# Moving the split weight tiles of an encoder kernel to other byte positions in SBUF

## The chip, the core and the metric

The kernel runs on one core of one Trainium2 chip. The metric is the device time of one launch in microseconds. TensorE multiplies, VectorE (DVE) and ScalarE (ACT) do the elementwise work, GpSimd (POOL) does a few small operations and issues one kind of transfer, and SyncE (SP) issues nearly all transfers from HBM. SBUF, the on-chip memory, has 128 partitions; a tile has the same byte position in each of them, and these positions are what the change is about.

## The reference

The reference is a trunk of two layers over 256 tokens of width 2048. Each layer normalises, projects the tokens, runs 12 token-mixing heads and 4 heads of cross-attention into 256 memory tokens side by side, projects their joined output back, and adds it. Then comes a dense squared-ReLU MLP of width 8192. All of it is in float32.

```python
for i in range(2):
    n = rms_norm(h, attn_norm[i])
    z = n @ (a_w_in if i == 0 else b_w_in)          # 2048 -> 5120 or 3072
    mix = neighbourhood_attention(...) if i == 0 else gqa_block_attention(...)
    km, vm = split(m @ w_mem_kv[i])                  # m: normalised memory tokens
    cross = memory_attention(qm, km, vm)
    h = h + concat([mix, cross]) @ w_o[i]
    n = rms_norm(h, mlp_norm[i])
    h = h + square(relu(n @ w_up[i])) @ w_down[i]    # 2048 -> 8192 -> 2048
return rms_norm(h, final_norm)
```

## The kernel before

**Products in three.** TensorE multiplies in float32r here, which keeps fewer bits than float32. So each factor is split into a high part and the rest: `split` has ScalarE copy the source into a float32r tile (L301) and VectorE subtract the copy from the source (L302). A product of two such pairs is three matmuls, high by high, high by low and low by high, summed in PSUM. Every weight comes from HBM as raw float32 (`raw`, `raw_U`, `raw_T`, `b`, `t`), is split into two tiles, and is then read by TensorE.

**What streams and what stands still.** A matmul loads one operand of 128 by 128 into the array, where it stands still, and streams the other through it. There are four kinds of product:

- *S products* (`s_products`, L221 to L223): the weights stand still, and the 256 tokens of the input (`nT` or `memT`) stream. 256 columns each.
- *Up products* (`u_products`, L696 to L698): the same shape, with the MLP's input `hT` streaming and the weights `uh`, `ul` standing still. 3 × 2048 matmuls.
- *M products* (`m_products`, L209 to L213): the weights stream in 512 columns, and the input (`nT`, `memT`, `cat`, or the squared activations `a_p`) stands still.
- *Down products* (`run` in `down_grains`, L810 to L812): the activations `a_s` stand still and the weights stream, in 512 columns. Seven eighths of the down projection are done in pairs with seven products in place of eight: the first three take the split of `b` (`bh`, `bl`), the other four that of `t` (`th`, `tl`), whose blocks VectorE and an accumulating transfer from POOL's queue (L790) make by adding and subtracting. The last eighth (`plain_grains`) goes as M products.

The next operand to stand still is loaded while the present one is multiplied (PEld in the profile).

**Order.** The work is a list of grains, each with steps to load, to prepare and to split some grains ahead. `add_mlp` puts an up grain and a down grain in turn, so that VectorE's and ScalarE's splits run beside TensorE's matmuls. What comes out, for most of the MLP, is an alternation on TensorE: 48 up matmuls (two halves of 24, from two tiles of `uh` and `ul`), then 21 down matmuls. A scheduler orders the instructions of each engine when the program is built.

**Where the tiles stand.** A pool places its tiles one behind the other. `new_half` makes the split tiles of the S and M products from the pool `ring`: four of `hi`, four of `lo`, each `HALF + 64` floats long, of which a window of `HALF` floats (4096 bytes) is used. The window begins `STILL_AT` bytes into the tile for S products and at 0 for M products. `half_of_side` does the same for `uh` and `ul` from the pool `side`, two of each, with the window at `place` bytes: 0 for up products, `MOVING_AT` for the M products that use these tiles. A tile of `HALF + 64` floats is 4352 bytes, which is 256 more than a multiple of 512, so neighbours stand 256 bytes apart modulo 512. The pool `mlp` holds `z`, `c`, `a`, `bh`, `bl`, `th`, `tl`.

Of the kernel before, what the change touches and what calls it, by code (L numbers as in the profile page):

```python
# [10 lines left out]
F32 = mybir.dt.float32  # L11
F32R = mybir.dt.float32r
# [5 lines left out]
P = 128  # L18
# [16 lines left out]
HALF = CH // 2  # L35
# [3 lines left out]
STEPS = PK // 2  # L39
GUARD = 3  # L40

MOVING_AT = 160

STILL_AT = 64
MASKED = -1e30


# [27 lines left out]
def encoder_kernel(ctx: ExitStack, tc: tile.TileContext, t: dict, out: bass.AP):  # L75
    nc = tc.nc
# [3 lines left out]
    def opened(name, side="left", space=None, bufs=1):  # L80
        kw = {"space": space} if space else {}
        manager = tc.tile_pool(name=name, bufs=bufs, side=side, reuse_waits="tile", **kw)
        pools[name] = manager, manager.__enter__()
        return pools[name][1]
# [35 lines left out]
    for j in range(8):  # L120
        s = slice(j * 512, (j + 1) * 512)
        nc.sync.dma_start(mem0[:, s], t["memT"][:, s])
        if j % 2 == 0:
            s = slice(j * 256, (j + 2) * 256)
# [20 lines left out]
    def halves_of(w):  # L145

        tiles = {}

        def load():
            tiles["raw"] = loaded(w.src, "U")  # L150

        def prep_early(hf):
            tiles[hf] = half_of_side(tiles["raw"], hf, MOVING_AT)

        def prep(hf):
            if hf == 0:
                tiles["raw"] = at.ring.tile([P, CH], F32, tag="raw", bufs=3, name="raw")
                nc.sync.dma_start(tiles["raw"], w.src)
            tiles[hf] = new_half(w.kind)
            split(*tiles[hf], tiles["raw"][:, hf * HALF : (hf + 1) * HALF])  # L160

        def run(hf):
            if hf == 0:
                w.start(w)
            hi, lo = tiles.pop(hf)
            if w.kind == "S":
                s_products(w, hf * (KT // 2), KT // 2, hi, lo)
            else:
                for i in range(NT):
                    m_products(w, w.first + 2 * hf, 2, i, hi, lo, w.begins and hf == 0, w.last and hf == 1)  # L170

        def after():
            if w.last:
                w.done(w)
            if w.early == "last":
                to_work()

        if w.early:
            return [Grain(lambda: run(0), None, load, None, lambda: prep_early(0), SOON),
                    Grain(lambda: run(1), after, None, None, lambda: prep_early(1), SOON)]  # L180
        return [Grain(lambda: run(0), None, None, None, lambda: prep(0)),
                Grain(lambda: run(1), after, None, None, lambda: prep(1))]

    def new_half(kind):
        s = slice(STILL_AT // 4, STILL_AT // 4 + HALF) if kind == "S" else slice(0, HALF)
        return tuple(at.ring.tile([P, HALF + 64], F32R, tag=n, bufs=4, name=n)[:, s] for n in ("hi", "lo"))

    pin = tc.keep_in_program_order

# [109 lines left out]
    def split(dst_hi, dst_lo, src):  # L299

        first = nc.scalar.activation(dst_hi, src, AF.Copy)  # L301
        return first, nc.vector.tensor_tensor(dst_lo, src, dst_hi.bitcast(F32), op=ALU.subtract)  # L302
# [396 lines left out]

    def half_of_side(raw, hf, place=0):  # L700
        s = slice(place // 4, place // 4 + HALF)
        tiles = tuple(at.side.tile([P, HALF + 64], F32R, tag=n, bufs=2, name=n)[:, s] for n in ("uh", "ul"))
        box.setdefault("splits", []).append(split(*tiles, raw[:, hf * HALF : (hf + 1) * HALF]))
        return tiles

    def loaded(src, tag):
        raw = at.side.tile([P, CH], F32, tag=tag, bufs=2, name=f"raw_{tag}")
        nc.sync.dma_start(raw, src)
        return raw

    def up_grains(layer, part, m):
        own = {}

        def load():
            own["raw"] = loaded(t[f"w_up{layer}"][part * PK + m], "U")

        def prep(hf):
            own[hf] = half_of_side(own["raw"], hf)

        def run(hf):  # L720
            if hf == 0:
                if part == 0:
                    own["ps"] = at.acc.tile([P, 512], F32, tag="acc", name="ps_u")[:, :SEQ]
                else:
                    if part == 1 and m == 0:
                        closed("ps_att", "ps_acc")
                        at.sums = opened("ps_sums", space=bass.MemoryType.PSUM)
                        box["ps"] = {}
                    own["ps"] = at.sums.tile([P, 512], F32, tag="up", name="ps_u")[:, :SEQ]
            u_products(own["ps"], hf * (KT // 2), KT // 2, *own.pop(hf))  # L730

        def after():
            if part == 0 and m == 0:
                closed("cat", "ring")
                at.mlp = opened("mlp")
                box["z"] = [at.mlp.tile([P, 4, 512], F32, tag=f"z{q}", name=f"z{q}") for q in range(2)]
                box["z_set"] = set()
            squared(layer, part, m, own["ps"])

        return [Grain(lambda: run(0), None, load, None, lambda: prep(0), SOON),  # L740
                Grain(lambda: run(1), after, None, None, lambda: prep(1), SOON)]

    def squared(layer, part, m, ps):
# [23 lines left out]
    def down_grains(layer, part, n, begins, ends):  # L767

        q, j = part % 2 ^ n // STEPS, n % STEPS
        own = {}  # L770

        def load():
            src = t[f"w_pair{layer}"][(part * 2 + q) * STEPS + j]
            own["b"] = at.side.tile([P, 3 * 512], F32, tag="b", bufs=2, name="b")
            nc.sync.dma_start(own["b"], src[:, : 3 * 512])
            own["t"] = at.side.tile([P, 4, 512], F32, tag="T", bufs=2, name="t")
            nc.sync.dma_start(own["t"][:, 0, :], src[:, 3 * 512 :])

        def behind(fn):

            return (lambda: past(fn, box["splits"][-4])) if part == 0 and n < 2 else fn

        def block(k):

            return own["b"][:, k * 512 : (k + 1) * 512]

        def pre():
            s = own["t"]
            nc.vector.tensor_tensor(s[:, 1, :], s[:, 0, :], block(0), op=ALU.add)  # L789
            nc.gpsimd.dma_start(s[:, 0, :], block(1), accum_op=ALU.add)  # L790

        def prep_first():
            own["first"] = tuple(at.mlp.tile([P, 3 * 512], F32R, tag=x, name=x) for x in ("bh", "bl"))
            split(*own["first"], own["b"])

        def prep_second():
            s = own["t"]
            nc.vector.tensor_tensor(s[:, 2, :], s[:, 1, :], block(1), op=ALU.add)
            nc.vector.tensor_tensor(s[:, 3, :], s[:, 2, :], block(2), op=ALU.add)
            own["second"] = tuple(at.mlp.tile([P, CH], F32R, tag=x, name=x) for x in ("th", "tl"))  # L800
            split(*own["second"], s.rearrange("p a b -> p (a b)"))

        def run(which, products):
            hi, lo = own.pop(which)
            a = box["a", part, j]
            for name, ai, bi in products:
                if begins:
                    box["ps"][name] = at.sums.tile([P, 512], F32, tag=name, name=name)
                ps, s = box["ps"][name], slice(bi * 512, (bi + 1) * 512)
                nc.tensor.matmul(ps, a[:, 0, ai, :], hi[:, s], start=begins, stop=False)  # L810
                nc.tensor.matmul(ps, a[:, 0, ai, :], lo[:, s], start=False, stop=False)  # L811
                nc.tensor.matmul(ps, a[:, 1, ai, :], hi[:, s], start=False, stop=ends)  # L812

        def after(products):
            if ends:
                for name, _, _ in products:
                    taken(q, name)

        def after_second():
            after(SECOND)  # L820
            if ends:
                box["z_set"].add(q)
            if ends and (part, n) in FOLDS:
                folded(q)

        return [Grain(lambda: run("first", FIRST), lambda: after(FIRST), load, behind(pre), behind(prep_first), SOON),
                Grain(lambda: run("second", SECOND), after_second, None, None, behind(prep_second), SOON)]

# [35 lines left out]
    def plain_grains(layer, nb):  # L864
# [4 lines left out]
        own = {}  # L869
# [3 lines left out]

        def prep(c, hf):
            if c == 0:
                own[c, hf] = half_of_side(own[0], hf, MOVING_AT)
            else:
                own[c, hf] = tuple(at.mlp.tile([P, HALF], F32R, tag="bt"[hf] + x, name=f"{x}_p") for x in "hl")
                split(*own[c, hf], own[1][:, hf * HALF : (hf + 1) * HALF])
# [351 lines left out]
```

## Time and profile before

Three runs took 2053.01, 2053.34 and 2054.17 us, so the median is 2053.34. The page and the views are of one profiled execution.

| | before |
|---|---|
| median of the runs | 2053.34 us |
| span of the profiled execution | 2050.6 us |
| TensorE busy | 2028.0 us (99%) |
| weight loads busy | 1835.2 us (89%) |
| VectorE busy | 1657.1 us (81%) |
| ScalarE busy | 1242.0 us (61%) |
| GpSimd busy | 120.2 us (6%) |
| granted TensorE clock, mean | 0.998 |

The span runs from the first to the last instruction; what lies around it is not in the profile. A row of the groups names line, engine, operation, what is written and what is read, shapes and count; behind the bar stand the busy time in us, the mean of one in ns, and the idle time ahead of the group with what ended it. A row of the waits names who waited for whom: us in total, how often, and the longest. In the timeline a row is one instruction (or a few alike, with their count), with its start in us, its duration, the engine and the line. Matmuls are pipelined: one starts well before the one ahead of it has ended. The pace is therefore the difference between starts. In the view of stretches each row gives, behind the stretch and its length, the busy time and count of TensorE, weight loads, VectorE, ScalarE and GpSimd, then the granted clock, the busy share of the DMA engines and GB/s.

### The profile page before, as it was taken

What the parts mean: (1) busy time and instruction counts of PE and PEld (TensorE: products, weight loads), DVE (VectorE), ACT (ScalarE), POOL (GpSimd) and SP (SyncE); (2) the same over time, 40 slices, a digit from 0 to 9 for tenths busy, and PEclk for the clock granted to TensorE, in tenths of its full rate; (3) what the DMA queues carried; (4) which work ended last, traced back from release to release, by engine and by line L of the source; (5) the groups of instructions that cost most, each with busy time, mean ns of one, the idle gap of its engine ahead of it and who ended that gap; (6) DMA issues with size and microseconds to landing.
All of it is one profiled execution on the core that took longest, in us unless ns stands there. A gap on an engine that the chain in (4) does not pass through costs nothing.

```text
span 2050.6 us, 32620 instructions
## 1 busy us (share of the span) xinstructions
PE 2028.0 (99%) x13092; PEld 1835.2 (89%) x13092; DVE 1657.1 (81%) x2025; ACT 1242.0 (61%) x1616; POOL 120.2 (6%) x144
## 2 busy tenths in 40 slices
PE   8999999999999999999999999999999999999998
PEld 7899999889999999999988888889999999999996
DVE  6766666558998999989896667657989999999896
ACT  6645454556666666666655557556666666666664
POOL 0000000000000000000000001000000000000000
PEclk9999999999999999999999999999999999999999
DMA  7755555727777777777765554537878787777773
GB/s 280 284 190 180 189 175 178 275 86 224 234 228 232 218 238 230 220 234 226 232 219 204 178 180 144 195 115 224 242 223 237 215 243 220 232 226 228 231 220 134
DMA packets 93431, 433.84 MB, mean 212 GB/s; under 512 B 10464, under 2 KB 12128, under 8 KB 60128
## 3 DMA queue, kind: packets, MB, share of 16 engines
q1 hardware_dynamic: 75888, 399.25, 57.7%
q0 software_dynamic: 16816, 31.46, 8.7%
q8 instruction: 102, 1.67, 0.3%
q10 hardware_dynamic: 576, 1.05, 0.1%
q14 instruction: 49, 0.40, 0.1%
HBM read 398.17 MB, written 4.19 MB: 196 GB/s over the span
## 4 chain that ended last, share of the span: by engine, by line
PE 94%; DVE 3%; DMA 1%; ACT 1%; issue 1%; SPq 0%; POOLq 0%; POOL 0%; DVEq 0%; ACTq 0%
PE ps_u L698 11%; PE ps_u L696 11%; PE ps_u L697 11%; PE p L810 8%; PE p L811 8%; PE p L812 8%; PE ps_m L209 8%; PE ps_m L212 8%; PE ps_m L213 8%; PE ps_s L221 3%; PE ps_s L223 3%; PE ps_s L222 3%; DVE ul L302 1%; PE pt_a L378 1%; DVE tl L302 1%
## 5 line engine op out<-in xcount | busy, mean ns | idle before, releaser
L698 PE MATMUL ps_u<-hT,ul 128*128 128x256 f32 x2048 | 568.1, 278 | 2.4 <-DVE ul L302 2.3
L696 PE MATMUL ps_u<-hT,uh 128*128 128x256 f32 x2048 | 568.0, 277 | 0.1
L697 PE MATMUL ps_u<-hT,uh 128*128 128x256 f32 x2048 | 567.4, 277 | 0.0
L301 ACT ACTIVATE uh<-raw_U 128x1024 fp32r<-128x1024 f32 x278 | 294.6, 1061 | 303.5 <-PE ps_u L697 281.0
L302 DVE TENSOR_TENSOR lo<-raw,hi 128x1024 fp32r<-128x1024 f32 (+1 forms) x224 | 266.3, 1195 | 162.1 <-ACT hi L301 160.0
L698 PEld LDWEIGHTS ps_u<-hT,ul 128*128 128x128 f32 x2048 | 385.5, 188 | 5.2 <-DVE ul L302 4.2
L696 PEld LDWEIGHTS ps_u<-hT,uh 128*128 128x128 f32 x2048 | 384.9, 188 | 5.5 <-ACT uh L301 0.5
L697 PEld LDWEIGHTS ps_u<-hT,uh 128*128 128x128 f32 x2048 | 384.4, 188 | 4.6
L302 DVE TENSOR_TENSOR ul<-raw_U,uh 128x1024 fp32r<-128x1024 f32 x278 | 337.2, 1218 | 37.5 <-ACT uh L301 37.4
L301 ACT ACTIVATE hi<-raw 128x1024 fp32r<-128x1024 f32 (+1 forms) x224 | 231.8, 1040 | 215.9 <-PE ps_m L213 121.1
L301 ACT ACTIVATE th<-t 128x2048 fp32r<-128x2048 f32 x112 | 215.2, 1921 | 125.4 <-PE p L812 111.8
L302 DVE TENSOR_TENSOR tl<-t,th 128x2048 fp32r<-128x2048 f32 x112 | 256.1, 2286 | 26.4 <-ACT th L301 25.8
L302 DVE TENSOR_TENSOR bl<-b,bh 128x1536 fp32r<-128x1536 f32 x112 | 196.0, 1750 | 0.3 <-ACT bh L301 0.2
L811 PE MATMUL p<-tl,a_s 128*128 128x512 f32 x448 | 177.2, 395 | 0.0
L812 PE MATMUL p<-th,a_s 128*128 128x512 f32 x448 | 174.4, 389 | 0.0
L301 ACT ACTIVATE bh<-b 128x1536 fp32r<-128x1536 f32 x112 | 166.2, 1484 | 10.1 <-PE p L812 4.0
L810 PE MATMUL p<-th,a_s 128*128 128x512 f32 x448 | 166.1, 395 | 0.0
L790 POOL DMA_DIRECT2D t<-b x112 | 97.1, 867 | 1166.0 <-DVE t L789 593.6
L811 PE MATMUL p<-bl,a_s 128*128 128x512 f32 x336 | 131.0, 390 | 0.2 <-DVE bl L302 0.2
L812 PE MATMUL p<-bh,a_s 128*128 128x512 f32 x336 | 131.1, 390 | 0.0
L789 DVE TENSOR_TENSOR t<-t,b 128x512 f32<-128x512 f32 x112 | 77.2, 689 | 64.1 <-DMA t<-in_w_pair 52.5
L223 PE MATMUL ps_s<-nT,lo 128*128 128x256 f32 x448 | 124.9, 279 | 0.0
(233 smaller groups left out, 3813.4 us busy)
## 6 DMA issues: line engine op xcount, KB each, us to landing
raw_U<-in_w_up SPq DMA_DIRECT2D x128, 1024.0 KB, 6.6
b<-in_w_pair SPq DMA_DIRECT2D x112, 768.0 KB, 4.5
raw<-in_w_o SPq DMA_DIRECT2D x32, 1024.0 KB, 5.1
t<-in_w_pair SPq DMA_DIRECT2D x112, 256.0 KB, 3.5
t<-b POOLq DMA_DIRECT2D x112, 256.0 KB, 6.8
raw<-in_w_b SPq DMA_DIRECT2D x21, 1024.0 KB, 5.0
raw<-in_w_av SPq DMA_DIRECT2D x12, 1024.0 KB, 5.1
raw<-in_w_aq SPq DMA_DIRECT2D x12, 1024.0 KB, 5.0
```

Of the source, the lines that this page charges most:

```text
L209: first = nc.tensor.matmul(w.ps[i], ah, hi[:, s], start=st, stop=False)
L212: nc.tensor.matmul(w.ps[i], ah, lo[:, s], start=False, stop=False)
L213: nc.tensor.matmul(w.ps[i], al, hi[:, s], start=False, stop=sp)
L223: nc.tensor.matmul(ps, lo[:, s], acts[:, k, :SEQ], start=False, stop=k == KT - 1)
L301: first = nc.scalar.activation(dst_hi, src, AF.Copy)
L302: return first, nc.vector.tensor_tensor(dst_lo, src, dst_hi.bitcast(F32), op=ALU.subtract)
L696: nc.tensor.matmul(ps, hi[:, s], acts[:, k, :SEQ], start=k == 0, stop=False)
L697: nc.tensor.matmul(ps, hi[:, s], acts[:, k, SEQ:], start=False, stop=False)
L698: nc.tensor.matmul(ps, lo[:, s], acts[:, k, :SEQ], start=False, stop=k == KT - 1)
L810: nc.tensor.matmul(ps, a[:, 0, ai, :], hi[:, s], start=begins, stop=False)
L811: nc.tensor.matmul(ps, a[:, 0, ai, :], lo[:, s], start=False, stop=False)
L812: nc.tensor.matmul(ps, a[:, 1, ai, :], hi[:, s], start=False, stop=ends)
```

## The change

The split tiles become `HALF + P` floats (4608 bytes, nine times 512), so that all tiles of a name have the same position modulo 512. The windows begin at new offsets. Two tiles that nothing reads, `apart0` (32 bytes) and `apart` (256 bytes), shift what stands behind them in the pool `mlp`. [...]

No instruction is added, removed or reordered on any engine; PE, DVE and ACT wait for the same semaphore values. On SP's and POOL's queues a few transfers around the change from the first MLP to the second layer's attention wait for other values, since the tiles that they overwrite lie elsewhere.

```diff
-MOVING_AT = 160
-
-STILL_AT = 64
+MOVING_AT = 256
+EARLY_AT = 416
+PLAIN_AT = 448
+STILL_AT = 320
...
         def prep_early(hf):
-            tiles[hf] = half_of_side(tiles["raw"], hf, MOVING_AT)
+            tiles[hf] = half_of_side(tiles["raw"], hf, EARLY_AT)
...
     def new_half(kind):
-        s = slice(STILL_AT // 4, STILL_AT // 4 + HALF) if kind == "S" else slice(0, HALF)
-        return tuple(at.ring.tile([P, HALF + 64], F32R, tag=n, bufs=4, name=n)[:, s] for n in ("hi", "lo"))
+        first = (STILL_AT if kind == "S" else MOVING_AT) // 4
+        s = slice(first, first + HALF)
+        return tuple(at.ring.tile([P, HALF + P], F32R, tag=n, bufs=4, name=n)[:, s] for n in ("hi", "lo"))
...
     def half_of_side(raw, hf, place=0):
         s = slice(place // 4, place // 4 + HALF)
-        tiles = tuple(at.side.tile([P, HALF + 64], F32R, tag=n, bufs=2, name=n)[:, s] for n in ("uh", "ul"))
+        tiles = tuple(at.side.tile([P, HALF + P], F32R, tag=n, bufs=2, name=n)[:, s] for n in ("uh", "ul"))
...
                 at.mlp = opened("mlp")
+                at.mlp.tile([P, 8], F32, tag="apart0", bufs=1, name="apart0")
...
         def prep_first():
+            if part == 0 and n == 0:
+                at.mlp.tile([P, 64], F32, tag="apart", bufs=1, name="apart")
             own["first"] = tuple(at.mlp.tile([P, 3 * 512], F32R, tag=x, name=x) for x in ("bh", "bl"))
...
             if c == 0:
-                own[c, hf] = half_of_side(own[0], hf, MOVING_AT)
+                own[c, hf] = half_of_side(own[0], hf, PLAIN_AT)
...
-    nc = _bacc.Bacc("TRN2", target_bir_lowering=False, num_devices=1)
+    nc = _bacc.Bacc("TRN2", target_bir_lowering=False, num_devices=1, dynamic_dma_scratch_size=8192)
```

The two built programs give these byte positions modulo 512 (where two stand, the tiles of a name alternate):

| operand | before | after |
|---|---|---|
| `hT`, input of the up products | 160 | 160 |
| `nT`, `memT`, `cat`, input of the S and M products | 128 | 128 |
| `uh`, `ul` for up products | 224 and 480 | 480 |
| `hi`, `lo` for S products | 192 and 448 | 448 |
| `hi`, `lo` (and early `uh`, `ul`) for M products | 128 and 384 | 384 |
| `bh`, `bl`, `th`, `tl` | 128 | 416 |
| activations `a_s`, `a_p` | 128 | 160 |

From these follows the distance between what streams and what is loaded next to stand still, modulo 512:

| where | before | after |
|---|---|---|
| inside up products, inside S products | 448 and 192 | 192 |
| inside M products | 0 and 256 | 256 |
| inside down products | 0 | 256 |
| from down to up products | 416 (at a few places 160) | 448 |
| from up to down products | 32 | 0 |
| from M to S products | 192 | 448 |
| from S to M products | 0 | 0 |
| from M to up products | 416 and 160 | 416 |
| inside the attention's score and value products | 0 | 0 |
| between S products and attention products | 160 in, 32 out | 160 in, 32 out |

All positions within a chunk differ by multiples of 512 bytes, so one number holds for a whole tile.

## The prediction

> **What bounds the kernel now.** I read the head of the page first, then TensorE's waits, then TensorE's groups by shape, and last its timeline, matmul by matmul.
>
> ```profile
> span 2050.6 us, 32620 instructions
> PE 2028.0 (99%) x13092; PEld 1835.2 (89%) x13092; DVE 1657.1 (81%) x2025; ACT 1242.0 (61%) x1616; POOL 120.2 (6%) x144
> PE ps_s L221 <- ACT hi L301: 7.0, 1, 7.0
> PE ps_u L698 <- DVE ul L302: 2.3, 5, 0.8
> PE p L810 <- ACT c L750: 2.1, 2, 1.1
> ```
>
> TensorE is busy for 99% of the span, and the largest of its waits for other engines is one of 7.0 us. No stall is left that a different start of a transfer could shorten by more than that. What remains is the pace of 13,092 matmuls. The change touches nothing else: the instructions of every engine stand in the same order in both programs, and TensorE's, VectorE's and ScalarE's waits are the same one by one.
>
> The profiled execution has a span of 2050.6 us. The three timed runs have a median of 2053.34, so 2.7 us lie around the span; I add differences to the median.
>
> ```profile
> L698 PE MATMUL ps_u<-hT,ul 128*128 128x256 f32 x2048 | 568.1, 278 | 2.4 <-DVE ul L302 2.3
> L810 PE MATMUL p<-bh,a_s 128*128 128x512 f32 x336 | 108.4, 390 | 2.1 <-ACT c L750 2.1
> L811 PE MATMUL p<-tl,a_s 128*128 128x512 f32 x448 | 177.2, 395 | 0.0
> ```
>
> The mean of one (278, 390, 395 ns) is no pace, since each matmul starts before the last has ended. The pace is read from starts in the timeline. There are 112 steps of the paired down product (L810 with bh: 336 rows, three a step). In TensorE's order 96 of them alternate as 48 up matmuls of 256 columns, then 21 down matmuls of 512; the other 16 are split differently. One such block:
>
> ```profile
> 511.00 0.39 PE L812 MATMUL p<-bh,a_s 128*128 128x512 f32 x1
> 511.23 0.28 PE L696 MATMUL ps_u<-hT,uh 128*128 128x256 f32 x1
> 511.83 0.28 PE L698 MATMUL ps_u<-hT,ul 128*128 128x256 f32 x1
> 512.96 0.28 PE L696 MATMUL ps_u<-hT,uh 128*128 128x256 f32 x1
> 513.98 0.28 PE L696 MATMUL ps_u<-hT,uh 128*128 128x256 f32 x1
> 515.00 0.28 PE L696 MATMUL ps_u<-hT,uh 128*128 128x256 f32 x1
> ```
>
> From 511.23 to 511.83 five matmuls take 0.60 us, 120 ns each. From 512.96 to 513.98 nine take 1.02 us, 113.3 ns each, and from 513.98 to 515.00 nine again take 1.02. (*Distance*, here and below: the byte position of the operand that streams, less that of the next one to stand still, modulo 512, as the table of the change gives it.) The first 24 of the 48 read the weight tile that stands at 224, the last 24 (from 513.98) the one at 480. So a settled run has one pace, **113.3 ns**, at distance 448 and at distance 192. There is a second pace, with nothing in the waits to explain it:
>
> ```profile
> 707.20 0.28 PE L698 MATMUL ps_u<-hT,ul 128*128 128x256 f32 x1
> 709.78 0.28 PE L696 MATMUL ps_u<-hT,uh 128*128 128x256 f32 x1
> 712.61 0.39 PE L810 MATMUL p<-th,a_s 128*128 128x512 f32 x1
> 715.36 0.84 PE L810 MATMUL p<-bh,a_s 128*128 128x512 f32 x3
> 717.40 0.28 PE L696 MATMUL ps_u<-hT,uh 128*128 128x256 f32 x1
> 722.87 0.40 PE L810 MATMUL p<-th,a_s 128*128 128x512 f32 x1
> 725.66 0.84 PE L810 MATMUL p<-bh,a_s 128*128 128x512 f32 x3
> 727.70 0.28 PE L696 MATMUL ps_u<-hT,uh 128*128 128x256 f32 x1
> ```
>
> From 707.20 to 712.61, 46 up matmuls take 5.41 us: **117.6 ns** each, in the 22 ahead of 709.78 (2.58 us, distance 448) as in the 24 behind it (2.83 us, distance 192). This is the slow pace; it holds until something disturbs it. It also shows in the mean of one, which TensorE's groups give as 281 ns in a stretch of this run (707.3 to 712.4 us) and as 276 in one of the next (718.3 to 722.6):
>
> ```profile
> L697 PE MATMUL ps_u<-hT,uh 128*128 128x256 f32 x15 | 4.2, 281 | 0.0
> L697 PE MATMUL ps_u<-hT,uh 128*128 128x256 f32 x13 | 3.6, 276 | 0.0
> ```
>
> The next run, 717.40 to 722.87, takes 5.47 us for 48 at the usual pace. The down run shows the reverse: its first twelve matmuls take 2.75 us behind these 46 (712.61 to 715.36) and 2.79 behind the usual 48 (722.87 to 725.66), and nine settled ones 2.04 us (725.66 to 727.70), 226.7 ns each. So twelve cost 0.03 or 0.07 us more than the settled 2.72.
>
> **The change, part by part.** *Weights at one distance.* All weight tiles of the up and the S products come to distance 192, which half of them have today; all of the M products come to 256, which half have. Both halves keep the same pace in the rows above, the fast and the slow. I cost this at nothing. Taken the other way, as if the first half's slow start (0.60 us against 5 × 113.3 = 0.567) were due to 448, it would be worth 0.03 us × 96 = 3 us. But the same start is there at 192:
>
> ```profile
> 440.46 0.28 PE L696 MATMUL ps_u<-hT,uh 128*128 128x256 f32 x1
> 441.06 0.28 PE L698 MATMUL ps_u<-hT,ul 128*128 128x256 f32 x1
> ```
>
> This is the first up run of the layer, whose first tile stands at 480: again 0.60 us for five.
>
> *Down blocks at 256.* They go from 0 to 256. The trace has no paired down product at 256, but M products of 512 columns stand at 0 and at 256 and settle alike, so the settled pace stays. The bounds for the excess at the start of a down run are 0.07 us as now and 0.03 as behind the 46.
>
> *The step from one kind to the other.* This is what really moves. From down to up, the distance between the data that is streaming and the first weights loaded under it goes from 416 to 448; from up to down it goes from 32 to 0. In other words, from an odd multiple of 32 to a multiple of 64. Today only S and M products meet at multiples of 64, from M to S at 192 (448 in the change) and from S to M at 0:
>
> ```profile
> 99.23 0.39 PE L213 MATMUL ps_m<-hi,memT 128*128 128x512 f32 x1
> 100.14 0.28 PE L221 MATMUL ps_s<-nT,hi 128*128 128x256 f32 x1
> 102.96 0.28 PE L221 MATMUL ps_s<-nT,hi 128*128 128x256 f32 x1
> 225.34 0.28 PE L221 MATMUL ps_s<-nT,hi 128*128 128x256 f32 x1
> 231.00 0.28 PE L221 MATMUL ps_s<-nT,hi 128*128 128x256 f32 x1
> 78.35 0.40 PE L209 MATMUL ps_m<-hi,memT 128*128 128x512 f32 x1
> 81.10 0.61 PE L209 MATMUL ps_m<-hi,memT 128*128 128x512 f32 x2
> ```
>
> The four M products from 99.23 run settled (0.91 us). The S products then take 2.82 us for 24, 117.5 ns each, from the first one on: the slow pace, without the kick of five uneven starts after which an up run falls to 113.3. After the M to S step at 225.34, 48 take 5.66 us: 117.9 ns. From S to M, 78.35 to 81.10, twelve take 2.75 us, the short start. The slow pace of an S product ends when another product breaks in:
>
> ```profile
> 312.69 0.28 PE L221 MATMUL ps_s<-nT,hi 128*128 128x256 f32 x1
> 313.87 0.28 PE L222 MATMUL ps_s<-nT,hi 128*128 128x256 f32 x1
> 313.99 0.28 PE L352 MATMUL sc_ps<-kT,qT 128*128 128x256 f32 x1
> 314.58 0.28 PE L221 MATMUL ps_s<-nT,hi 128*128 128x256 f32 x1
> 315.26 0.28 PE L221 MATMUL ps_s<-nT,hi 128*128 128x256 f32 x1
> ```
>
> Ten in 1.18 us before the score product at 313.99, six in 0.68 (113.3 ns) from 314.58 on; its steps in and out are at 160 and 32, odd multiples of 32. If the kick comes from such a step, the change takes it away at the 96 places where it helps. Each up run then begins at the slow pace, which every run has at first, and stays there: 48 × 5.41/46 = 5.645 us, and the down run behind it takes the 4.79 us of 712.61 to 717.40. A block becomes 10.435 us instead of 10.30 (717.40 to 727.70): +0.135, × 96 = **+13.0 us**. The 16 split steps stay as they are.
>
> *Half the scratch for POOL's transfers.* POOL issues one accumulating transfer a block:
>
> ```profile
> t<-b POOLq DMA_DIRECT2D x112, 256.0 KB, 6.8
> 600.00:700.00 100.00, 100.00 (x669) 91.36 (x668) 91.71 (x102) 66.38 (x69) 8.73 (x10) 1.00 0.79 232
> ```
>
> It lands in 6.8 us, a block takes 10.30, so two are hardly ever under way: nothing. [...]
>
> *New places for the other engines.* In the stretch from 600 to 700 us TensorE is busy throughout, VectorE for 91.7%. A slower or faster split from a tile in another place is hidden up to about 8%; beyond that TensorE waits at L698 and L811. I take nothing. The few changed waits are of weight and memory loads on SP's and POOL's queues around the return to the attention layout, behind 1067 us, where the queued DMAs have no TensorE wait that shows: nothing, or a microsecond either way.
>
> [...]
>
> **The rivals.** *Clean.* Steps at 0 and 448 start no disturbance and the fast pace holds from the start: 48 × 113.3 = 5.44 us, and a down run of 4.79 with the short start of S to M. 10.23 us a block, −0.07 × 96 = −6.7 us: 2046.6. For it: the S to M step at 0 shows the short start. Against it: both kinds of run that follow one of 512 columns begin near the slow pace, those at 511.23 and 440.46 with 120 ns and that at 100.14 with 117.5.
>
> *Half of it.* The up run keeps its kick, because its own tiles stand 32 bytes past a multiple of 64 and S's do not, and only the down run starts shorter: 10.26 us, −0.04 × 96 = −3.8 us: 2049.5, which is −0.19%.
>
> [...]
>
> *A lower floor.* [...] Half of the up and the M products stand at the new distances already and are at 113.3 and 226.7, so I give this hardly a chance. In rows, a further step down as large as that from the slow pace to the fast one, 4.3 ns, for the three groups of 2048 up matmuls would give 26 us: 2027.
>
> **How the numbers follow.** A measurement of this kernel can tell about 0.2%, 4.1 us, from no change. Slow pace after every step: 0.42, 2053.3 + 13.0 = **2066**, its own range 2060 (half the blocks) to 2068. Other losses (a ring too short, splits too slow): 0.05, above 2058. Clean: 0.25, 2047. Lower floor: 0.03. Half of it: 0.12, and nothing: 0.13, both inside 0.2%. So slower 0.47, same 0.25, faster 0.28. Cases of both signs hold most of the chance, so the range runs from the clean case, 2045, to the slow one, 2068.
>
> **What would show it.** If I am right, 48 up matmuls take 5.6 us in nearly every block, the mean of L696 to L698 rises from 278 to about 281 ns, the first twelve down matmuls take 2.75 us, and TensorE's waits stay as they are. Up runs of 5.44 to 5.47 us prove the step theory wrong; if then the down runs are at 4.79, half of it stands. [...] A first up run after M products (440.46, at 416 before and after) that keeps its kick while the others lose it would be the strongest sign for the step.

## The result and the profile after

| | before | after |
|---|---|---|
| median of the runs | 2053.18 us (2052.26 to 2054.17) | 2065.22 us (2064.62 to 2065.88) |
| span of the profiled execution | 2050.6 us | 2062.8 us |

The ratio is 1.0059, with a 95% interval of 1.0048 to 1.0071: slower by 12.0 us. The head of the profile's page after, TensorE's largest wait for ScalarE and its largest for VectorE, and two groups of TensorE:

```profile
span 2062.8 us, 32621 instructions
PE 2040.2 (99%) x13092; PEld 1852.4 (90%) x13092; DVE 1660.0 (80%) x2025; ACT 1240.8 (60%) x1616; POOL 120.3 (6%) x144
PE ps_s L223 <- ACT hi L303: 7.0, 1, 7.0
PE ps_u L700 <- DVE ul L304: 2.1, 4, 0.8
L700 PE MATMUL ps_u<-hT,ul 128*128 128x256 f32 x2048 | 574.7, 281 | 2.1 <-DVE ul L304 2.1
L816 PE MATMUL p<-tl,a_s 128*128 128x512 f32 x448 | 175.4, 391 | 0.0
```

The one instruction more is a semaphore wait on POOL, among the changed waits of its queue. The span grew by 12.2 us and TensorE's busy time by 12.2 us. The waits are the ones of before (7.0 and 2.1 us, where 7.0 and 2.3 stood). So the loss is all pace, and the groups say where: the up products rose from 278 to 281 ns, the down products with tl fell from 395 to 391. The timeline of TensorE shows one block (each row a start, a duration, the line; the rows kept are the first, sixth and 25th up matmul, the first and 13th down matmul, and the next block's first):

```profile
511.36 0.28 PE L698 MATMUL ps_u<-hT,uh 128*128 128x256 f32 x1
511.95 0.28 PE L700 MATMUL ps_u<-hT,ul 128*128 128x256 f32 x1
514.18 0.28 PE L698 MATMUL ps_u<-hT,uh 128*128 128x256 f32 x1
517.01 0.40 PE L815 MATMUL p<-th,a_s 128*128 128x512 f32 x1
519.76 0.84 PE L815 MATMUL p<-bh,a_s 128*128 128x512 f32 x3
521.80 0.28 PE L698 MATMUL ps_u<-hT,uh 128*128 128x256 f32 x1
```

The first 24 up matmuls take 2.82 us and the next 24 take 2.83, so 5.65/48 = 117.7 ns each from the first to the last: the slow pace, without the kick, the few uneven starts after which an up run falls to 113.3 ns (the first five take 0.59 us, 118 each). The first twelve down matmuls take 2.75 us, the last nine 2.04. The block takes 10.44 us where 10.30 stood, and 96 × 0.14 = 13.4 us. The microsecond between that and the growth of the span lies outside the blocks: added up from their starts over the whole profiled execution, the down runs there are 0.9 us shorter than before, and the up runs there 0.2 us.

One up run did not change. It is the first of the layer, which follows M products, at a distance of 416 in both kernels:

```profile
440.38 0.28 PE L698 MATMUL ps_u<-hT,uh 128*128 128x256 f32 x1
440.98 0.28 PE L700 MATMUL ps_u<-hT,ul 128*128 128x256 f32 x1
442.23 0.28 PE L699 MATMUL ps_u<-hT,uh 128*128 128x256 f32 x1
```

Five in 0.60 us, as from 440.46 to 441.06 before, and then eleven in 1.25 us, 113.6 ns each. It kept its kick while the 96 runs behind down products lost theirs.

### The profile page after: what moved, and what is told of

Same layout as the page of the kernel before. It is cut to its first block, busy times and chain, and to the rows that moved or that the text cites. A ratio compares the mean times of both kernels' runs of the same rounds, so it can differ in the third digit from the quotient of the medians.

```text
span 2062.8 us, 32621 instructions
## 1 busy us (share of the span) xinstructions
PE 2040.2 (99%) x13092; PEld 1852.4 (90%) x13092; DVE 1660.0 (80%) x2025; ACT 1240.8 (60%) x1616; POOL 120.3 (6%) x144
## 4 chain that ended last, share of the span: by engine, by line
PE 97%; DVE 1%; ACT 1%; issue 1%; DMA 0%; SPq 0%; POOLq 0%; POOL 0%; ACTq 0%
PE ps_u L700 11%; PE ps_u L698 11%; PE ps_u L699 11%; PE p L815 9%; PE p L816 9%; PE p L817 9%; PE ps_m L211 8%; PE ps_m L214 8%; PE ps_m L215 8%; PE ps_s L223 3%; PE ps_s L225 3%; PE ps_s L224 3%; PE pt_a L380 1%; PE pt_n L321 1%; DVE ul L304 0%
## 5 line engine op out<-in xcount | busy, mean ns | idle before, releaser
L700 PE MATMUL ps_u<-hT,ul 128*128 128x256 f32 x2048 | 574.7, 281 | 2.1 <-DVE ul L304 2.1
L698 PE MATMUL ps_u<-hT,uh 128*128 128x256 f32 x2048 | 574.3, 280 | 0.2
L699 PE MATMUL ps_u<-hT,uh 128*128 128x256 f32 x2048 | 573.9, 280 | 0.0
L223 PE MATMUL ps_s<-nT,hi 128*128 128x256 f32 x448 | 124.8, 279 | 0.0
```

Source lines behind the costliest of these rows:

```text
L223: nc.tensor.matmul(ps, hi[:, s], acts[:, k, :SEQ], start=k == 0, stop=False)
L698: nc.tensor.matmul(ps, hi[:, s], acts[:, k, :SEQ], start=k == 0, stop=False)
L699: nc.tensor.matmul(ps, hi[:, s], acts[:, k, SEQ:], start=False, stop=False)
L700: nc.tensor.matmul(ps, lo[:, s], acts[:, k, :SEQ], start=False, stop=k == KT - 1)
```

## The experiments

The theory to be tried: the step from one kind of product to the other decides whether an up run falls to the fast pace, and the change moved the steps. Its rivals: the scratch (`dynamic_dma_scratch_size`), the distances inside a kind, or the other parts of the change make the loss. In each verdict the ratio is against the kernel before on the same chip. "Place" is the byte position of the down tiles (`a_s`, `bh` and the rest) modulo 256. It fixes both steps, since `hT` stays at 160 and the up weights at 224 modulo 256. The unread tile stands ahead of all of the pool `mlp`, so `z` and `c`, which VectorE and ScalarE use, move with the down tiles. In the versions of the kernel before, all instructions, their order and what they wait for are those of the kernel before.

**The change with its old steps.** Everything of the change stays, but the down tiles go back by 32 bytes.

```diff
-PLAIN_AT = 448
+PLAIN_AT = 416
-                at.mlp.tile([P, 8], F32, tag="apart0", bufs=1, name="apart0")
```

> The change without the 32-byte tile apart0 (and the plain products' window 32 bytes lower, so that they stay at 256): the distances inside the runs stay 192 and 256 as in the change, the steps go back to 416 (down to up) and 32 (up to down). Step theory: the kick is back, 48 up matmuls take 5.47 to 5.48 us and 21 down ones 4.82, and the time is that of before, 2052 to 2055 us. If the distances inside the runs (or the smaller scratch) made it slower, it stays at 2063 to 2067.

Measured: 2052.58 us, ratio 1.0002 (0.9992 to 1.0011). The timeline of TensorE, one block:

```profile
717.73 0.28 PE L698 MATMUL ps_u<-hT,uh 128*128 128x256 f32 x1
718.33 0.28 PE L700 MATMUL ps_u<-hT,ul 128*128 128x256 f32 x1
723.21 0.40 PE L814 MATMUL p<-th,a_s 128*128 128x512 f32 x1
725.99 0.84 PE L814 MATMUL p<-bh,a_s 128*128 128x512 f32 x3
728.03 0.28 PE L698 MATMUL ps_u<-hT,uh 128*128 128x256 f32 x1
```

The kick is back (five in 0.60 us), the up run is at 5.48, the nine settled down matmuls at 2.04, the block at 10.30. Weights at one distance, down blocks at 256 and half the scratch together cost nothing that the runs can tell (0.1% either way).

**The steps alone.** The kernel before, with its down tiles moved by 32 bytes. The last line of the diff keeps the distance inside the M products at the end of the down projection as it was; the versions below that move the tiles by 64 to 224 bytes are made in the same way, with another number of floats and another offset.

```diff
                 at.mlp = opened("mlp")
+                at.mlp.tile([P, 8], F32, tag="apart0", bufs=1, name="apart0")
-                own[c, hf] = half_of_side(own[0], hf, MOVING_AT)
+                own[c, hf] = half_of_side(own[0], hf, MOVING_AT + 32)
```

> The kernel before with the down tiles and the activations moved together by 32 bytes (a tile of 32 bytes ahead of them), and the plain products' window with them: inside the runs everything stays at 192/448, 0/256 and 0; only the steps change, to 448 (down to up) and 0 (up to down). Step theory: the slow pace after every step, 48 up matmuls in 5.65 us, 2064 to 2067 us. If distances inside the runs are the cause, no change: 2052 to 2055.

Measured: 2065.69 us, ratio 1.0062 (1.0047 to 1.0077). TensorE's timeline, an up run and the down run's first:

```profile
721.19 0.28 PE L696 MATMUL ps_u<-hT,uh 128*128 128x256 f32 x1
726.85 0.40 PE L811 MATMUL p<-th,a_s 128*128 128x512 f32 x1
```

5.66 us for 48. An unread tile of 32 bytes ahead of the down tiles, with that window moved along, makes the whole loss.

**The scratch alone.** The kernel before with this part of the change only, which the prediction calls half the scratch.

```diff
-    nc = _bacc.Bacc("TRN2", target_bir_lowering=False, num_devices=1)
+    nc = _bacc.Bacc("TRN2", target_bir_lowering=False, num_devices=1, dynamic_dma_scratch_size=8192)
```

> The kernel before with 8192 bytes of scratch for POOL's transfers, nothing else (all tiles move down by 8192 bytes together). Step theory: no change, 2052 to 2055 us, up runs of 5.48 us. [...]

Measured: 2052.49 us, ratio 1.0003 (0.9993 to 1.0014). The page's row of POOL's transfers:

```profile
t<-b POOLq DMA_DIRECT2D x112, 256.0 KB, 6.7
```

They land in 6.7 us, 6.8 before. This part costs nothing that the runs can tell.

**Steps at another odd multiple of 32.** The prediction took the kick to come from a distance that is an odd multiple of 32. Moved by 64 bytes, both steps are at 480, which is one.

> As the second kernel, but moved by 64 bytes: steps at 480 (down to up) and 480 (up to down), again odd multiples of 32, but other ones than before. If it is only whether the step is a multiple of 64, the kick is there again and the time is that of before, 2051 to 2056 us. If the exact distance 416 matters, it is slow, 2064 to 2067, or lies between.

Measured: 2068.29 us, ratio 1.0076 (1.0061 to 1.0091). TensorE's timeline:

```profile
716.42 0.40 PE L811 MATMUL p<-th,a_s 128*128 128x512 f32 x1
719.18 0.84 PE L811 MATMUL p<-bh,a_s 128*128 128x512 f32 x3
721.23 0.28 PE L696 MATMUL ps_u<-hT,uh 128*128 128x256 f32 x1
726.88 0.39 PE L811 MATMUL p<-th,a_s 128*128 128x512 f32 x1
```

The up run takes 5.65 us, slow throughout. The down run shown, behind 46 up matmuls, takes 2.76 for its first twelve; behind 48 it is 2.77, nearly the long start of before. So an odd multiple of 32 is not enough for the kick: the rule that the prediction had given the steps is wrong.

**Three more places.** Moved by 192, 128 and 224 bytes.

> The kernel before with the down tiles and activations moved by 192 bytes: steps at 96 (down to up) and 352, which is 96 modulo 256 (up to down). So far a step into the up run at 416 kicked it to the fast pace, and steps at 448 and 480 did not. Parity theory (odd multiples of 32 kick, with 480 as an exception): 48 up matmuls in 5.48 us, about 2053 us. Theory that only distances near 160 modulo 256 kick (160 does, 192 and 224 do not): 5.65 us, 2063 to 2069.

> The same, moved by 128 bytes: steps at 32 (down to up) and 416 (up to down). After attention products the trace of before has S runs that enter at 32 and fall to 113 ns. Theory that 32 kicks as 160 does (anything from 32 to 160 modulo 256): 5.48 us, 2051 to 2056. Theory that it is 160 alone: 5.65 us, 2063 to 2069.

> The same, moved by 224 bytes: steps at 128 (down to up) and 320, which is 64 modulo 256 (up to down). Parity theory: a multiple of 64 does not kick, 5.65 us and 2063 to 2069. Theory of a range that ends between 160 and 192: it kicks, 5.48 us, 2050 to 2056.

Measured: steps at 96, 2049.07 us, ratio 0.9982 (0.9972 to 0.9992); step into the up run at 32, 2048.13, 0.9976 (0.9965 to 0.9986); at 128, 2062.81, 1.0052 (1.0031 to 1.0072). TensorE's timeline with steps at 96, a down run and the up run behind it:

```profile
721.43 0.39 PE L811 MATMUL p<-th,a_s 128*128 128x512 f32 x1
724.19 0.84 PE L811 MATMUL p<-bh,a_s 128*128 128x512 f32 x3
726.24 0.28 PE L696 MATMUL ps_u<-hT,uh 128*128 128x256 f32 x1
726.81 0.28 PE L698 MATMUL ps_u<-hT,ul 128*128 128x256 f32 x1
731.69 0.39 PE L811 MATMUL p<-th,a_s 128*128 128x512 f32 x1
```

Five in 0.57 us and 48 in 5.45: the up run is fast from its first matmul, with no kick. The same view with the step at 32:

```profile
716.63 0.28 PE L696 MATMUL ps_u<-hT,uh 128*128 128x256 f32 x1
717.22 0.28 PE L698 MATMUL ps_u<-hT,ul 128*128 128x256 f32 x1
722.09 0.39 PE L811 MATMUL p<-th,a_s 128*128 128x512 f32 x1
724.84 0.84 PE L811 MATMUL p<-bh,a_s 128*128 128x512 f32 x3
726.89 0.28 PE L696 MATMUL ps_u<-hT,uh 128*128 128x256 f32 x1
```

A kick (the first five take 0.59 us, the other 43 then 4.87, 113.3 ns each), 5.46 for 48, and a down run of 4.80 with the short start. The block is 10.26 us: −0.04 × 96 = −3.8, measured −4.5. And at 128:

```profile
720.55 0.28 PE L696 MATMUL ps_u<-hT,uh 128*128 128x256 f32 x1
726.21 0.40 PE L811 MATMUL p<-th,a_s 128*128 128x512 f32 x1
728.94 0.84 PE L811 MATMUL p<-bh,a_s 128*128 128x512 f32 x3
```

5.66 us for 48, slow. So 160 is not alone, and there is no range from 32 to 160; that multiples of 64 are slow and odd multiples of 32 fast, with 480 as an exception, fits these three.

**The inside of the down run at 480.** The activations move by 32 bytes, the split weights stay. So the step into the up run is at 416 as before, the one into the down run at 0, and the two operands inside a down run stand 480 apart in place of 0.

```diff
+                at.mlp.tile([P, 8], F32, tag="apart0", bufs=1, name="apart0")
...
+            if part == 0 and n == 0:
+                at.mlp.tile([P, 120], F32, tag="apart", bufs=1, name="apart")
...
-                own[c, hf] = half_of_side(own[0], hf, MOVING_AT)
+                own[c, hf] = half_of_side(own[0], hf, MOVING_AT + 32)
```

> The kernel before with the activations moved by 32 bytes and the down blocks left where they were: the step into the up run stays at 416, the step into the down run becomes 0, and the distance inside the down runs becomes 480, an odd multiple of 32. If each step acts by itself and the distance inside the down runs is free: 48 up matmuls in 5.48 us and 21 down ones in 4.79, 96 x 0.036 = 3.5 us less than before, about 2049. If inside distances of 512-column runs matter, the 21 down matmuls take over 4.83 us; at 4 ns a matmul, as 113 to 118, that is 96 x 21 x 4 ns = 8 us more, 2061.

Measured: 2077.95 us, ratio 1.0126 (1.0109 to 1.0143). A group of the page, whose mean of one (396 ns, 395 before) hides the change of pace, and behind it rows of TensorE's timeline:

```profile
L814 PE MATMUL p<-tl,a_s 128*128 128x512 f32 x448 | 177.4, 396 | 0.0
717.97 0.39 PE L813 MATMUL p<-th,a_s 128*128 128x512 f32 x1
720.77 0.86 PE L813 MATMUL p<-bh,a_s 128*128 128x512 f32 x3
722.87 0.28 PE L696 MATMUL ps_u<-hT,uh 128*128 128x256 f32 x1
724.28 0.28 PE L696 MATMUL ps_u<-hT,uh 128*128 128x256 f32 x1
```

The first twelve down matmuls take 2.80 us and the last nine 2.10, 233 ns each in place of 226.7: this down run never settles. And the up run behind it is slow (twelve in 1.41 us, 117.5 ns each) although its step is at 416, at which it had its kick before. The two runs together take 5.65 + 4.90 = 10.55 us, and 96 × 0.25 = 24 of the 25.3 us lost; both forecasts were too low. So a distance inside a run can cost after all, and the step into the up run does not decide its pace by itself. Two readings are left. One is that the pace of the down run ahead counts too. The other is that the pace of the up run goes with the place of the activations, and so with the step into the down run: that is 0 here, as in the change, whose up runs are slow. In every other version here both steps move together, so no run tells these readings apart.

**The two places still missing.** Moved by 96 and 160 bytes.

> The kernel before with the down tiles moved by 96 bytes: the step from down to up goes from 416 to 0, the one from up to down from 32 to 448; the distances inside stay. So far the up runs came out fast behind steps at 32, 96 and 160 (modulo 256) and slow behind 128, 192 and 224. Theory 'an odd multiple of 32 is needed, but not every one is enough': 0 is slow, 48 up matmuls in 5.65 us, some +0.17 us a block, and the time between 2062 and 2069. Rival 'each step has a pace of its own, without a rule by multiples of 64': 0 can kick as well, 5.45 to 5.48 us and 2046 to 2054.

> The kernel before with the down tiles moved by 160 bytes: down to up 64, up to down 384. Theory 'an odd multiple of 32 is needed': slow, 5.65 us for 48 and 2062 to 2069. Rival without such a rule: 64 stands between 32 and 96, both of which came out fast, so 5.45 us and 2046 to 2051.

Measured: step into the up run at 0, 2061.03 us, ratio 1.0041 (1.0027 to 1.0055); at 64, 2064.33, 1.0058 (1.0044 to 1.0071). TensorE's timeline with the step at 0:

```profile
719.48 0.28 PE L696 MATMUL ps_u<-hT,uh 128*128 128x256 f32 x1
725.13 0.39 PE L811 MATMUL p<-th,a_s 128*128 128x512 f32 x1
727.85 0.84 PE L811 MATMUL p<-bh,a_s 128*128 128x512 f32 x3
729.89 0.28 PE L696 MATMUL ps_u<-hT,uh 128*128 128x256 f32 x1
```

And with the step at 64:

```profile
721.29 0.28 PE L696 MATMUL ps_u<-hT,uh 128*128 128x256 f32 x1
726.95 0.39 PE L811 MATMUL p<-th,a_s 128*128 128x512 f32 x1
729.67 0.84 PE L811 MATMUL p<-bh,a_s 128*128 128x512 f32 x3
```

Both up runs are slow (5.65 and 5.66), and both down runs are settled from the first: twelve in 2.72 us. That an odd multiple of 32 is needed holds for these blocks. The two blocks are alike, yet the times are 3.3 us apart and the profiled spans 4.3 (2059.2 and 2063.5). Of the 4.3 us, 3.4 lie in up runs outside the 96 blocks. Ten runs of 46 up matmuls take 5.23 us with the step at 0 and 5.42 with the step at 64, which is 1.9 us, and the long up runs of 361 early in each layer's MLP take 44.45 and 45.45 against 45.39 twice, 0.9 us. Why they do stays open.

**The change at a better place.** The changed kernel with the first unread tile 128 bytes long, and the version with the step at 32 once more beside it.

```diff
-PLAIN_AT = 448
+PLAIN_AT = 32
-                at.mlp.tile([P, 8], F32, tag="apart0", bufs=1, name="apart0")
+                at.mlp.tile([P, 32], F32, tag="apart0", bufs=1, name="apart0")
```

> The changed kernel with everything it has (one distance inside a kind, 256 inside the down runs, half the scratch), but with the first unread tile 128 bytes long in place of 32, so that the step from down to up stands at 32 and the one from up to down at 416 (160 modulo 256), as in the version with steps 32. Theory 'the steps alone decide, and only modulo 256': as that version, 2048.1 within 1.5, up runs of 5.46 us and down runs of 4.79. Rival 'the one distance inside matters once the steps are good': more than 1.5 us away from it on either side.

> The version of the kernel before with steps at 32 and 416, once more beside the others. If its gain of 4.5 us is real, it comes out at 2048 again, ratio 0.998 with an interval below 1. If it was chance, the interval holds 1.

Measured: 2047.79 us, ratio 0.9980 (0.9971 to 0.9988), and 2046.92, 0.9975 (0.9964 to 0.9986). Both are faster than both kernels of this case, and 0.9 us apart. The distances inside a kind add nothing that these runs can tell. The profiled execution of the first took longer than its median (span 2052.0); TensorE's waits in it have a row that the kernel before lacks:

```profile
PE p L816 <- DVE tl L304: 3.8, 5, 1.0
```

VectorE's second split of `t` came late five times. With blocks of 10.26 us and VectorE busy for 91.3 to 92.0% from 500 to 800 us, TensorE sometimes catches up with it. That this is why the faster versions scatter more (2046.19 to 2053.82 in eleven runs here, 2064.62 to 2065.88 in four of the change; 2051.15 to 2055.77 in seventeen of the kernel before) is argued, not shown.

All eight places at steps of 32 bytes, with the up and down runs as their timelines above have them (before: as in the prediction):

| place | step into up | step into down | 48 up | 12 down | ratio |
|---|---|---|---|---|---|
| 128 (before) | 160 | 32 | 5.47, kick | 2.79 | 1 |
| 160 (the change) | 192 | 0 | 5.65, slow | 2.75 | 1.0059 |
| 192 | 224 | 224 | 5.65, slow | 2.76 | 1.0076 |
| 224 | 0 | 192 | 5.65, slow | 2.72 | 1.0041 |
| 0 | 32 | 160 | 5.46, kick | 2.75 | 0.9976 |
| 32 | 64 | 128 | 5.66, slow | 2.72 | 1.0058 |
| 64 | 96 | 96 | 5.45, fast at once | 2.76 | 0.9982 |
| 96 | 128 | 64 | 5.66, slow | 2.73 | 1.0052 |

The steps are given modulo 256, since the paces tell nothing of a difference of 256: the halves of an up run at 224 and at 480 run alike, and the first up run of an MLP, 17 matmuls, enters at 416 in the first layer of the kernel before and at 160 in the second, and takes 1.97 us in both. No two runs differ in a step of the blocks by 256 alone.

With inner distances of 0 or 256 for down and 448 or 192 for up, an up run of 48 behind 21 down matmuls is fast behind a step of 32, 96 and 160, and slow behind every multiple of 64 and behind 224. This holds for all such runs of the profiled executions, to 0.01 us, but for one up run in the changed kernel at the better place (5.62). In the kernel before, the only two up runs of 48 that do otherwise follow eleven down matmuls, not 21, and are fast at once (5.45).

The runs of 46 do not follow the table. Ten of the twelve come behind six down matmuls, with two up matmuls ahead of these. In the kernel before they enter at 416 like the runs of 48, yet nine of the ten are slow to their end (5.42 us, the prediction's run at 707.20 among them), while the two of 46 behind 19 down matmuls are fast (5.25). With the step at 0 all ten behind six down matmuls are fast, for example:

```profile
709.47 0.28 PE L698 MATMUL ps_u<-hT,ul 128*128 128x256 f32 x1
714.70 0.39 PE L811 MATMUL p<-th,a_s 128*128 128x512 f32 x1
```

46 in 5.23 us are 113.7 ns each, behind a multiple of 64. So the table is no rule for a step as such: it holds for one sequence of matmuls ahead of it, and with another sequence the same step can do the opposite.

## Why the prediction was right

- *TensorE's pace is the bound.* Right: the span and TensorE's busy time both grew by 12.2 us, and the waits stayed.
- *Weights at one distance, down blocks at 256, half the scratch, new places for the other engines: nothing.* Right. The change with its old steps is at 1.0002, the scratch alone at 1.0003.
- *The step moves, the up run loses its kick and stays slow, the down run starts shorter.* Right in place and size: 5.65 us against the 5.645 forecast, 2.75 for twelve as forecast, a block of 10.44 against 10.435. The sum of +13.0 us met +12.0. The first up run behind M products kept its kick, which the prediction had called the strongest sign, and 32 bytes alone give 1.0062.
- *"From an odd multiple of 32 to a multiple of 64".* Half wrong. In the 96 blocks all four multiples of 64 are slow, which is what this change needed. But of the odd multiples 224 is slow as well, 416 is slow when the down run stands at 480 inside, and runs of 46 are slow behind 416 and fast behind 0. That the sum came out is owed to the rows it was taken from, not to the rule. What spoke for the slow pace was the S products behind 192 and the first twelve M products behind 0, the very steps of the change modulo 256. The sizes, 5.41 us for 46 and 4.79, are those of the run at 707.20 and the down run behind it; that run itself enters at 416 and by the rule should have had the kick. There was luck in this: of the seven places other than that of before, five are slow, so a wrong rule had a good chance of naming a slow one.
- *The range*, 2045 to 2068, took in a gain as well as a loss, and the slow case had a chance of 0.42; that the time lies in it says little, the paces say more.
- *"The slow pace, which every run has at first".* Wrong: behind a step at 96 an up run starts at 113 ns.
- *Clean* (2047) did not happen, but what it described exists: an up run fast at once at 96, a down run settled at once behind 128 and 192. No place gives both fully. *Half of it* (kick kept, shorter down start, 2049.5) is what steps at 32 and 160 do, at 2048.1. *Nothing*, the case of 0.13 in which no distance counts and the time stays at 2053.3, falls: moving tiles that TensorE reads put the time between 0.9975 and 1.0126 of the kernel before, with the same matmuls in the same order. *A lower floor* was not seen; the settled 113.3 and 226.7 ns are the fastest paces in the timelines shown. *Other losses* (0.05) were not there, and no run shows a ring that is too short: with the scratch alone POOL's transfers landed in 6.7 us, 6.8 before, and among TensorE's waits in the changed kernel none is for `th` or `tl`.

What stays open is the reason inside TensorE. The runs name places and paces, and no record of the profile shows what a slow matmul waits for. Nor do they separate the distance to the up operands from the place of the down tiles itself, since `hT` and the up weights stood still in all of them, or, but for the version with 480 inside, the step into the up run from the step into the down run. That `z` and `c` moved too, and other engines' work on them slows TensorE, is not ruled out by a run of its own. Against it stands that the slow up runs are even: in the version moved by 32 bytes every start in all 96 comes 117 to 119 ns behind the last.

## What to carry to other kernels

Where TensorE is busy for 99% and starts come a few per cent apart for the same instruction, read the paces from the starts in the timeline, behind each kind of neighbour, before moving anything: the mean of one hides them (396 against 395 ns where the pace was 233 against 226.7). Byte positions in SBUF were then a thing to tune here (ratios of 0.9975 to 1.0076 over the eight places), those of the tiles read just ahead of the slow run; an unread tile of 32 to 224 bytes ahead of the tiles concerned tries a place and costs only its bytes, and eight places, 32 bytes apart, were the whole search here. It gained 0.2% over the kernel before. A rule guessed from two or three distances should be tried at the others before it is used to choose a layout, and held against every run of the trace that it is taken from: the kernel before already had runs behind 416 without the kick.

## What was not expected of the hardware

- Moving one group of tiles changes this kernel by 0.6% for 32 bytes (2065.69 us) and by 0.8% for 64 (2068.29), and by 1.3% when the operands inside the down run move against each other (2077.95).
- The down matmuls of 512 columns showed a second lasting pace too: 233 ns a matmul (nine in 2.10 us) in place of 226.7 (2.04), in the version where the streaming and the next standing operand are 480 apart.
- After at most its first five matmuls an up run of 48 has one pace to its end, across a change of weight tiles, in every block quoted here. Which of the two it is depends on what came before: in the kernel before, behind a step at 416, it was the fast one for 48 behind 21 down matmuls (5.48 us) and the slow one for nine of ten runs of 46 behind six (5.42 us).
